# A GLA layer with its MLP on one core: the MLP as eight interleaved rounds, all of the down projection by sums, engine orders set in the source

## The chip, the core and the metric

The kernel runs on one core of a Trainium2 chip. The metric is the device time of one execution in microseconds. A core has a matrix engine (PE, whose weight loads are listed apart as PEld), three engines for elementwise work (DVE, ACT, POOL), and DMA queues that are fed by SP, ACT and POOL. Each engine takes its own instructions in the order in which they stand in its stream, and waits on semaphores for the others. PE writes into eight banks of PSUM of 128 x 512 float32; everything else lies in SBUF.

## The reference, cut to what matters

One layer: a chunked gated linear attention as the mixer, then an MLP with squared ReLU, then a final norm. 256 tokens, width 2048, hidden width 8192, all in float32. The change concerns the MLP.

```python
def _sq_relu_mlp(h, w_up, w_down):
    a = jax.nn.relu(h @ w_up)
    return (a * a) @ w_down

h = x
h = h + _gla_mixer(_rmsnorm(h, gla_norm), ...)
h = h + _sq_relu_mlp(_rmsnorm(h, mlp_norm), w_up, w_down)   # 256x2048 @ 2048x8192, then @ 8192x2048
return _rmsnorm(h, final_norm)
```

## The kernel before, in words

**Split numbers.** Every float32 operand of a large product is split into a high part (a cast on ACT to float32r, line 109) and a low part (the rest, a subtraction on DVE, line 110). A product of two such operands is three matmuls: high with high, high with low, low with high. Each matmul has a stationary block of 128 x 128 and 256 moving columns; the text calls one such matmul a product step.

**The mixer** (lines 180 to 560) projects with `natural` (line 142) and `turned` (line 157), each a loop that loads a piece of a weight matrix on SP's queue, splits it and multiplies. Small jobs of other kinds wait in the deque `side` and are let in by `pump` (line 88), one for each piece. The last jobs before the MLP turn the tokens: `turn` (line 510) transposes two blocks of 128 columns through an auxiliary bank on PE, and ACT and DVE write the high and low part of the turned `h`. `add_h` (line 542) adds the output projection to `h`, `ssq_h`, `scale2` and `scale2_row` (lines 548, 568, 576) make the norm's factor for each token as a row: squares on ACT, sums on DVE, a power on POOL, a diagonal on DVE, two small matmuls on PE.

**The MLP** goes in four rounds (`ROUNDS = HID // D`, line 61), each over 2048 hidden columns. A round first makes the up projection in four groups of 512 hidden columns (`up`, line 597, by `turned`), then the down projection in two halves of 1024 output columns (`down`, line 626). Per round, up is 4 x 192 = 768 product steps.

The down projection saves products by sums of blocks: tokens fall in two blocks of 128, hidden rows in pairs of blocks, output columns in pairs of 256. For such a 2x2 by 2x2 block product seven products of sums of blocks do instead of eight (lines 610 to 612 make the sums of the activations, line 666 those of the weights, line 686 and 697 put the results together from the banks `b32`, `b74`, `b16`, `b50`). Before the change only the left 512 of each 1024 output columns go that way; the right 512 (`blocks`, bank `plain`) are multiplied plainly. One pair of hidden blocks then takes 24 plain steps and 21 by sums:

```python
            product(b16, left, at(A11), w0, right, last)
            blocks(0, w0)
            product(b32, right, at(A12), w1, right, last)
            product(b32, left, at(S4), w1, left, last)
            blocks(1, w1)
            product(b50, left, at(S1), wu, slice(0, T), last)
            product(b74, left, at(S3), wu, slice(T, 2 * T), last)
            product(b16, right, at(S2), wu, slice(2 * T, 3 * T), last)
            product(b74, right, at(A22), wu, slice(3 * T, G), last)
```

In the second half, pair 0 is multiplied plainly (`PLAIN`, line 624), 48 steps. The very last half of the last round is all plain, and its last six pieces are held back so that the first token block's output can leave early (`last_step`, `held`).

**What sets the order.** Tile's scheduler orders the instructions of each engine by its own estimate of time and puts in all semaphores. `issue_after` ties the side jobs to the pieces. Split weights live in five buffers of 1024 columns (`wpool`), raw ones in three.

Of the kernel before, what the change touches and what calls it, by code (L numbers as in the profile page):

```python
# [27 lines left out]
F32 = mybir.dt.float32  # L28
# [32 lines left out]
ROUNDS = HID // D  # L61
# [5 lines left out]
def tile_gla_mlp(ctx, tc, x, xt, cols, w_vg, w_in, w_gate, w_out, w_up, w_down, final_norm, out):  # L67
# [3 lines left out]
    big = ctx.enter_context(tc.tile_pool(name="big", bufs=2))  # L71
    mid = ctx.enter_context(tc.tile_pool(name="mid", bufs=1))
    wpool = ctx.enter_context(tc.tile_pool(name="wpool", bufs=5))
    tmp = ctx.enter_context(tc.tile_pool(name="tmp", bufs=2))
    st = ctx.enter_context(tc.tile_pool(name="st", bufs=4))
    acc_p = ctx.enter_context(tc.tile_pool(name="acc_p", bufs=6, space=bass.MemoryType.PSUM))
# [114 lines left out]
    ones = const.tile([P, P], F32, name="ones")  # L191
    nc.vector.memset(ones, 1.0)
    warm = aux_bank()
    for _ in range(WARM):
# [4 lines left out]
    ident = const.tile([P, P], F32, name="ident")  # L199
# [4 lines left out]
    zz = big.tile([P, 2, 8, T], F32, tag="C", name="zz")  # L204
    kab = big.tile([P, 2, 8, T], F32, tag="C", name="kab")
    xth, xtl = (
        big.tile([P, KT * ROW + 64], F32R, tag="A" + i, name="x" + i, bufs=1)[:, OFF : OFF + KT * ROW]
# [93 lines left out]
    vh = big.tile([P, NT, D], F32R, tag="B", name="vh")  # L301
    vl = big.tile([P, NT, D], F32R, tag="B", name="vl")
    gn = const.tile([P, NT, GR], F32, name="gn")
# [21 lines left out]
    dq = const.tile([P, 8, 2], F32, name="dq")  # L325
# [107 lines left out]
    at = big.tile([P, 2, HEADS, 3 * P + 64], F32R, tag="C", name="at")  # L433
# [43 lines left out]
    on = big.tile([P, NT, D], F32, tag="C", name="on")  # L477
# [48 lines left out]
    oth, otl = (big.tile([P, KT * T + 128], F32R, tag="B", name="ot" + i) for i in "hl")  # L526
# [31 lines left out]
    hth, htl = (big.tile([P, KT, T], F32R, tag="A" + i, name="h" + i, bufs=1) for i in "hl")  # L558
# [26 lines left out]
    side.extend([scale2, nothing, scale2_row])  # L585

    A11, A12, A21, A22, S3, S1, S2, S4 = range(8)  # L590
    KP = KT // 2
    work = mid.tile([P, 3 * G + T], F32, tag="qt", name="work")
    r2row = work[:, 3 * G :]
    work = work[:, : 3 * G].rearrange("p (b c) -> p b c", b=3)
    ends = mid.tile([P, 4, T], F32, tag="db", name="ends")

    def up(r, q, act):
        acc = turned(hth, htl, w_up, r * D + q * GT, even=() if q > 1 or r > 0 and q else (5,) if r == q == 0 else (0,))
        flush()
        f = work[:, 2].rearrange("p (f s) -> p f s", f=8)  # L600
        for b in range(2):
            s = tmp.tile([P, 2, T], F32, tag="t512", name="su", bufs=3)
            nc.vector.scalar_tensor_tensor(
                s, acc[b].rearrange("p (i t) -> p i t", i=2), 0.0, r2row.unsqueeze(1).to_broadcast([P, 2, T]),
                op0=ALU.max, op1=ALU.mult,
            )
            nc.scalar.activation(
                f[:, :4].rearrange("p (t i) s -> p i t s", t=2), s.rearrange("p i (t s) -> p i t s", t=2), AF.Square
            )
            sub = lambda o, x, y: nc.vector.tensor_tensor(o, x, y, op=ALU.subtract)  # L610
            sub(f[:, S3 : S1 + 1], f[:, A21 : A21 + 1].to_broadcast([P, 2, P]), f[:, A11 : A22 + 1 : 3])
            sub(f[:, S2], f[:, A11], f[:, S1])
            sub(f[:, S4], f[:, A12], f[:, S2])
            oh, ol = (act[q][:, b, i].rearrange("p f s -> p (f s)") for i in range(2))
            nc.scalar.copy(oh, work[:, 2])
            nc.vector.tensor_tensor(ol, work[:, 2], oh.bitcast(F32), op=ALU.subtract)

    def stationary(act, kp, f):
        return [act[kp // 2][:, kp % 2, i, f] for i in range(2)]

    def take(bank, t, lo, n):
        nc.vector.tensor_tensor(h[:, t, lo : lo + n], bank, h[:, t, lo : lo + n], op=ALU.add)  # L622

    PLAIN = ((), (0,))

    def down(r, half, act):

        c0 = half * G
        plain = [aux_bank(), aux_bank()] if half == 0 else acc_banks(2)
        b32, b74 = acc_banks(2) if half == 0 else [aux_bank(), aux_bank()]  # L630
        b16, b50 = acc_banks(2)
        left, right = slice(0, T), slice(T, 2 * T)
        used = set()

        def product(bank, o, a, w, m, last):

            for i, (x, y) in enumerate(((0, 0), (0, 1), (1, 0))):
                halves(bank[:, o], a[x], w[y][:, m], bank.name not in used, last and i == 2)
                used.add(bank.name)

        for kp in range(KP):
            last = kp == KP - 1
            at = lambda f: stationary(act, kp, f)
            w = rows(w_down, c0, G, r * D)
            blocks = lambda i, wi: [
                product(plain[t], slice(0, 512), at((A11, A21)[t] + i), wi, slice(512, G), last and i == 1) for t in range(NT)
            ]
            if kp in PLAIN[half]:
                for i in range(2):
                    wi = weights(w(2 * kp + i), G)  # L650
                    blocks(i, wi)
                    product(b32, slice(0, 512), at(A11 + i), wi, slice(0, 512), False)
                    product(b50, right, at(A21 + i), wi, left, False)
                    product(b74, right, at(A21 + i), wi, right, False)
                    pump()
                continue
            assert not raw_half
            pair = wpool.tile([P, 2 * WMAX], F32, tag="raw", name="raw", bufs=3)
            raw0, raw1 = pair[:, :WMAX], pair[:, WMAX:]
            w0 = weights(w(2 * kp), G, skip=T, raw=raw0)  # L660
            product(b16, left, at(A11), w0, right, last)
            blocks(0, w0)
            pump()
            w1 = weights(w(2 * kp + 1), G, raw=raw1)
            u = work[:, kp % 2].rearrange("p (f s) -> p f s", f=4)
            add = lambda o, x, y: nc.vector.tensor_tensor(o, x, y, op=ALU.add)

            both = pair[:, T : T + 2 * (WMAX - T)].rearrange("p (k c) -> p k c", k=2)[:, :, :T]
            add(u[:, :2], raw0[:, left].unsqueeze(1).to_broadcast([P, 2, T]), both)
            add(u[:, 2], u[:, 0], raw1[:, left])  # L670
            add(u[:, 3], u[:, 2], raw1[:, right])
            wu = parts(work[:, kp % 2], G, slots())
            product(b32, right, at(A12), w1, right, last)
            product(b32, left, at(S4), w1, left, last)
            blocks(1, w1)
            product(b50, left, at(S1), wu, slice(0, T), last)
            product(b74, left, at(S3), wu, slice(T, 2 * T), last)
            product(b16, right, at(S2), wu, slice(2 * T, 3 * T), last)
            product(b74, right, at(A22), wu, slice(3 * T, G), last)
            if not last:  # L680
                pump()
        flush()
        for t in range(NT):
            take(plain[t], t, c0 + 512, 512)

        tt = lambda o, x, y: nc.vector.tensor_tensor(o, x, y, op=ALU.subtract)
        nc.scalar.copy(ends[:, 1], b16[:, left])
        tt(ends[:, 3], ends[:, 1], b16[:, right])
        tt(ends[:, 0], b50[:, left], ends[:, 3])
        tt(ends[:, 2], ends[:, 3], b74[:, left])  # L690
        take(b32, 0, c0, 512)
        take(b74, 1, c0, 512)
        if PLAIN[half]:
            take(b50[:, right], 1, c0, T)
        for t in range(NT):
            hv = h[:, t, c0 : c0 + 512].rearrange("p (i s) -> p i s", i=2)
            nc.vector.tensor_tensor(hv, hv, ends[:, 0 : t + 2 : t + 1], op=ALU.add)

    for r in range(ROUNDS):
        act = [big.tile([P, 4 * G + 64], F32R, tag="BC"[q // 2], name="act")[:, OFF:-16] for q in range(D // GT)]  # L700
        act = [a.rearrange("p (b i f s) -> p b i f s", b=2, i=2, f=8) for a in act]
# [102 lines left out]
```

## Time and profile before

| what | us |
|---|---|
| median of 3 runs | 1073.75 (1073.36 to 1073.92) |
| the profiled execution, span from its first to its last instruction | 1071.9 |
| PE busy in that span | 1062.2 |
| DVE busy | 780.3 |
| ACT busy | 576.7 |
| POOL busy | 12.7 |
| read from HBM | 206.92 MB, mean rate 195 GB/s |

The MLP's first product of the up projection starts 382.3 us into the span. A page of the profile is read as follows. "PE busy" counts matmuls that overlap each other, so the rate at which they start is the measure, and it is taken from the chain of waits, which lists merged stretches with their count. Groups are named by line, engine, operation, what is written and read, and shape; "x" is the count, then come the time busy in all and the mean duration of one. Consecutive instructions of DVE or ACT overlap a little, which the merged rows of the timeline show. DMA rows give the size of a transfer and the median time from issue to landing.

### The profile page before, as it was taken

The page shows a single profiled execution, that of the slowest core. Times are in us where ns is not written, and L with a number is a line of the kernel's source. Part 1 is how long each engine was busy: PE and PEld are TensorE (multiplying, and loading weights), DVE is VectorE, ACT ScalarE, POOL GpSimd, SP SyncE. Part 2 cuts the span into 40 slices and gives each one's busy share as a digit, 9 for nine tenths or more (in the row PEclk, how much of TensorE's full clock was granted, in tenths as well). Part 3 has the DMA queues.
Part 4 walks back from the last instruction along what each step waited for, and adds up shares of the span by engine and source line. Part 5 has one row for each costly group of instructions (what it writes and reads, how often), then busy time and mean ns, then how long its engine had stood idle before and what let it go on. Part 6 is the DMA issues. An engine that isn't in the chain of part 4 may idle for free.

```text
span 1071.9 us, 21858 instructions
## 1 busy us (share of the span) xinstructions
PE 1062.2 (99%) x9273; PEld 1061.5 (99%) x9273; DVE 780.3 (73%) x1039; ACT 576.7 (54%) x698; POOL 12.7 (1%) x39
## 2 busy tenths in 40 slices
PE   9999999999999999999999999999999999999997
PEld 9999999999999999999999999999999999999997
DVE  6668644546555566789986689986779997678974
ACT  7675444546444454556554556564556554555652
POOL 0000000000000000000000000000000000000000
PEclk9999999999999999999999999999999999999999
DMA  9856664556545555546566655566654666654662
GB/s 329 314 174 201 193 191 146 164 154 195 195 162 194 192 166 195 196 160 227 204 207 203 191 188 197 197 210 223 198 193 163 222 208 206 194 194 173 228 227 79
DMA packets 81009, 210.43 MB, mean 196 GB/s; under 512 B 6752, under 2 KB 9824, under 8 KB 80784
## 3 DMA queue, kind: packets, MB, share of 16 engines
q1 hardware_dynamic: 79808, 206.86, 58.8%
q10 hardware_dynamic: 1104, 2.19, 0.6%
q8 instruction: 72, 1.18, 0.4%
q14 instruction: 25, 0.20, 0.1%
HBM read 206.92 MB, written 2.10 MB: 195 GB/s over the span
## 4 chain that ended last, share of the span: by engine, by line
PE 98%; issue 1%; DMA 0%; DVE 0%; ACT 0%; SPq 0%; POOLq 0%; POOL 0%; DVEq 0%; ACTq 0%
PE acc L140 43%; PE acc L169 41%; PE aux L140 12%; PE aux L515 1%; PE aux L442 1%; DMA raw<-in_w_vg 0%; PE aux L343 0%; SPq L132 0%; DVE vl L307 0%; DVE hf L763 0%; ACT sqf L716 0%; DVE h L622 0%; ACT vh L306 0%; ACT hi L109 0%; POOLq L800 0%
## 5 line engine op out<-in xcount | busy, mean ns | idle before, releaser
L110 DVE TENSOR_TENSOR lo<-raw,hi 128x1024 fp32r<-128x1024 f32 (+3 forms) x386 | 453.2, 1176 | 231.1 <-ACT hi L109 228.9
L109 ACT CAST hi<-raw 128x1024 fp32r<-128x1024 f32 (+3 forms) x386 | 390.4, 1013 | 397.7 <-PE acc L169 172.6
L169 PE MATMUL acc<-hh,hi 128*128 128x256 f32 x1024 | 283.3, 277 | 0.0
L169 PE MATMUL acc<-hh,lo 128*128 128x256 f32 x1024 | 283.2, 277 | 0.0
L169 PE MATMUL acc<-hl,hi 128*128 128x256 f32 x1024 | 283.1, 276 | 0.0
L140 PE MATMUL acc<-hi,act 128*128 128x256 f32 x1194 | 217.1, 276 | 0.0
L169 PEld LDWEIGHTS acc<-hh,hi 128*128 128x128 f32 x1024 | 192.4, 188 | 0.0
L169 PEld LDWEIGHTS acc<-hh,lo 128*128 128x128 f32 x1024 | 192.4, 188 | 0.0
L169 PEld LDWEIGHTS acc<-hl,hi 128*128 128x128 f32 x1024 | 192.4, 188 | 0.0
L140 PEld LDWEIGHTS acc<-hi,act 128*128 128x128 f32 x1194 | 180.0, 188 | 0.0
L140 PE MATMUL acc<-lo,act 128*128 128x256 f32 x597 | 142.4, 276 | 0.0
L140 PE MATMUL aux<-hi,act 128*128 128x256 f32 x716 | 135.1, 276 | 0.0
L140 PEld LDWEIGHTS aux<-hi,act 128*128 128x128 f32 x716 | 107.9, 188 | 0.0
L140 PEld LDWEIGHTS acc<-lo,act 128*128 128x128 f32 x597 | 101.9, 188 | 0.0
L140 PE MATMUL acc<-lo,xh 128*128 128x256 f32 x480 | 77.5, 280 | 0.0
L140 PE MATMUL aux<-lo,act 128*128 128x256 f32 x358 | 76.9, 276 | 0.0
L140 PE MATMUL acc<-hi,xl 128*128 128x256 f32 x480 | 76.8, 279 | 0.0
L140 PE MATMUL acc<-hi,xh 128*128 128x256 f32 x480 | 76.0, 281 | 0.6 <-ACT hi L109 0.6
L109 ACT CAST hi<-work 128x1024 fp32r<-128x1024 f32 x53 | 56.0, 1056 | 32.0 <-PE aux L140 11.9
L110 DVE TENSOR_TENSOR lo<-work,hi 128x1024 fp32r<-128x1024 f32 x53 | 64.7, 1220 | 10.6 <-ACT hi L109 9.2
L169 PE MATMUL acc<-xh,hi 128*128 128x256 f32 x256 | 70.9, 277 | 0.4 <-DVE vl L307 0.4
L169 PE MATMUL acc<-xl,hi 128*128 128x256 f32 x256 | 71.0, 277 | 0.0
(137 smaller groups left out, 1266.2 us busy)
## 6 DMA issues: line engine op xcount, KB each, us to landing
raw<-in_w_up SPq DMA_DIRECT2D x128, 512.0 KB, 4.6
raw<-in_w_down SPq DMA_DIRECT2D x128, 512.0 KB, 4.4
raw<-in_w_in SPq DMA_DIRECT2D x80, 512.0 KB, 4.9
raw<-in_w_out SPq DMA_DIRECT2D x32, 512.0 KB, 4.4
raw<-in_w_vg SPq DMA_DIRECT2D x13, 520.0 KB, 8.0
h<-in_x SPq DMA_DIRECT2D x4, 512.0 KB, 7.1
zz<-in_xt SPq DMA_DIRECT2D x2, 512.0 KB, 9.6
fb<-in_final_norm ACTq DMA_DIRECT2D x1, 1024.0 KB, 6.7
```

The costliest lines, as they stand in the source:

```text
L109: last_hi[0] = nc.scalar.copy(hi[:, s], raw[:, s])
L110: last_lo[0] = nc.vector.tensor_tensor(lo[:, s], raw[:, s], hi[:, s].bitcast(F32), op=ALU.subtract)
L140: nc.tensor.matmul(o[:, m], x, w[:, m], start=first and c == 0, stop=last, skip_group_check=True)
L169: nc.tensor.matmul(o, u[:, s], m[:, kt], start=kt == 0 and n == 0 and j % 2 == 0, stop=kt == KT - 1 and n == 2, skip_group_check=True,)
L442: nc.tensor.matmul(o, kab[:, k[0], c0 + c, k[1] : k[1] + P], q(qt[:, c0 + c]), start=c == 0, stop=c == 1)
L515: nc.tensor.transpose(b[:, i * T + t * P : i * T + (t + 1) * P], src[:, t, kt * P : (kt + 1) * P], ident)
```

## The change

The MLP is written anew; in the mixer only the homes of some tiles move. What it does:

- There are eight rounds over 1024 hidden columns each (`ROUNDS = HID // G`), and all output columns go by sums. The last round's down projection (the last 1024 hidden rows) is plain. A step `d` of the down projection covers 512 hidden rows and 512 output columns: 24 product steps on weights as loaded and one sum among them (`raws`) and 18 on further sums (`summed`), 42 in all, 56 times. The plain rest is 8 x 48.
- The up projection goes in 64 pieces `u` of 512 x 512 (48 product steps). Nine pieces (`LEAD`) go ahead; then each cycle is 48 steps of up for a later round, 24 and 18 of down. A cycle has 90 product steps.
- One of the four sums of weights is made by a DMA on POOL's queue that adds one part of a raw tile into another (`accum_op`); DVE makes the other three, and splits them.
- The banks `b32`, `b74`, `b16`, `b50` are filled by ACT from their homes in SBUF (`h`, `kept`) before a visit to a stretch of 512 output columns and emptied back afterwards. At the end `combine` puts the parts together.
- Every job is put into `plan` with a time in product steps, relative to the product that needs it; the plan is sorted by time and run inside `tc.manual_schedule()`, which keeps that order on every engine.
- The split weights live in three slots of 2048 columns, the raw ones in two buffers for up and two for down, in a pool that takes the mixer's place (`mixer.close()`), with waits tile by tile.
- `turn` for the second half of `h`, `scale2` and `scale2_row` are plan entries at 6, 15, 24, 33, 48 and 72, between the up pieces at 0, 48 and 96.

```diff
-ROUNDS = HID // D
+ROUNDS = HID // G
+LEAD = 9
+UP, RAWS, SUMS = 24, 24, 18
+CYCLE = 2 * UP + RAWS + SUMS
...
     add_h(acc, G)
-    side.extend([lambda q=q: turn(h, row_h, g2, q) for q in range(4, 8)])
+    mixer.close()
+    mlp = ctx.enter_context(tc.tile_pool(name="mlp", bufs=1, reuse_waits="tile"))
...
+    SLOTS, PLACE = 3, 2 * G + 64
+    raw_u = [room_for(2 * G, f"rawu{i}") for i in range(2)]
+    slot = [[room_for(PLACE, f"{x}{i}", F32R) for x in ("high", "low")] for i in range(SLOTS)]
+    raw_d = [room_for(2 * G, f"rawd{i}") for i in range(2)]
...
+    T0 = 2 * UP * LEAD
+    cycle = lambda d: T0 + CYCLE * d
...
+    banks = acc_banks(6)
+    for q in range(4, 8):
+        at(6 + 9 * (q - 4), lambda q=q: turn(h, row_h, g2, q))
+    at(48, scale2)
+    at(72, scale2_row)
+    at(74, lambda: banks.__setitem__(slice(0, 0), [aux_bank(), aux_bank()]))
+    at(100, fold)
...
+    UP_LOAD, UP_HI, UP_LO = 120, 75, 56
...
+            def high(key=key, to=to, raw=raw):
...
+                nc.scalar.copy(to[0], raw)
...
+            def low(key=key, to=to, raw=raw):
...
+                nc.vector.tensor_tensor(to[1], raw, to[0].bitcast(F32), op=ALU.subtract)
...
+        chunk(("u", u), p - UP_HI, p - UP_LO, p + 2 * UP, (p - UP_LOAD, load), raw, 0 if u in SAME else OFF)
...
+    for g in range(GROUPS):
+        u = 4 * g + 3
+        e = up_time(u) + 2 * UP
+        for i in range(2):
+            at(e + 6 + i, lambda g=g, b=i: scaled(g, b))
+        steps = [lambda g=g: differ(g)] + [lambda g=g, b=b, f=f: f(g, b) for b in range(2) for f in (act_high, act_low)]
...
+        at(t - 30, lambda d=d: fill(d, B32))
+        at(t - 24, lambda d=d: fill(d, B16))
+        for i, run in enumerate((
+            lambda o=old, l=last: empty(o, B32, l), lambda d=d: fill(d, B50),
+            lambda o=old, l=last: empty(o, B50, l), lambda d=d: fill(d, B74),
+            lambda o=old, l=last: empty(o, B16, l), lambda o=old, l=last: empty(o, B74, l),
+        )):
+            at(t + 34 + 5 * i, run)
...
+            for f, name, o, a in ((3, B16, left, A11), (1, B32, right, A12), (0, B32, left, S4), (2, B50, left, S1)):
+                product(d, name, o, stationary(d, b, a), [x[:, f] for x in w])
...
+        for f, name, o, a in ((0, B16, right, S2), (1, B74, right, A22), (2, B74, left, S3)):
+            for b in range(2):
+                product(d, name, o, stationary(d, b, a), [s[:, f, b] for s in sums_to])
...
+            nc.sync.dma_start(out=raw.rearrange("p (i c) -> p i c", i=4), in_=src)
+            nc.gpsimd.dma_start(out=view[:, :, 1, left], in_=view[:, :, 1, right], accum_op=ALU.add)
+
+        chunk(("d", d), p - 67, p - 50, p + RAWS, (p - 143, load), raw)
+
+        def adds():
...
+            add(sums[:, 0], view[:, :, 1, left], view[:, :, 0, left])
+            add(sums[:, 1], sums[:, 0], view[:, :, 0, right])
+            sub(sums[:, 2], sums[:, 0], view[:, :, 1, right])
...
+            nc.scalar.copy(sums_to[0][:, f], sums[:, f])
...
+            sub(sums_to[1], sums, sums_to[0].bitcast(F32))
...
+        at(p - 68, adds)
+        at(q - 74, lambda: high(slice(0, 2)))
+        at(q - 65, lambda: high(2))
+        at(q - 54, low)
+        at(p, lambda: raws(d))
+        at(q, lambda: summed(d))
...
+    place_chunks()
+    with tc.manual_schedule():
+        for _, _, run in sorted(plan, key=lambda x: x[:2]):
+            run()
...
-    for kt in range(KT):
-        k = kt - KT + ROOM
-        w = weights(rows(w_down, G, G, (ROUNDS - 1) * D)(kt), G, room=k >= 0 and [room[:, i, k, :] for i in range(2)])
-        if kt < KT - LAST:
+    for kt in range(X_STEPS):
+        k = kt - X_STEPS + ROOM
+        piece = slice(kt % 2 * G, (kt % 2 + 1) * G)
+        to = [room[:, i, k, :] for i in range(2)] if k >= 0 else [s[:, piece] for s in slot[(taken + kt // 2) % SLOTS]]
+        w = weights(plain_source(X_STEPS + kt), G, room=to, raw=raw_u[kt // 2 % 2][:, piece])
+        if kt < X_STEPS - LAST:
```

More of the change, by code (lines that the diff above doesn't have):

```diff
@@ L583, in scale2_row @@
         nc.scalar.copy(r2row, b[:, :T])
[L585 to L600, printed above, removed]
-        for b in range(2):
[L602 to L682, printed above, removed]
-        for t in range(NT):
[L684 to L697, printed above, removed]
@@ new lines, in act_low @@
+    def act_low(g, b):
+        sub(act_part(g, b, 1), forms[:, b, span(g)], act_part(g, b, 0).bitcast(F32))
+        done.add(("act", g, b))
+    for g in range(GROUPS):
+        u = 4 * g + 3
+        e = up_time(u) + 2 * UP
+        for i in range(2):
+            at(e + 6 + i, lambda g=g, b=i: scaled(g, b))
+        steps = [lambda g=g: differ(g)] + [lambda g=g, b=b, f=f: f(g, b) for b in range(2) for f in (act_high, act_low)]
+        if u < LEAD:
+            times = (e + 24, e + 33, e + 42, e + 43, e + 54)
+        else:
+            c = lambda n: cycle(u - LEAD + n)
+            if g % 2 == 0:
+                times = (c(1) + 54, c(2) + 33, c(2) + 54, c(3) + 33, c(3) + 54)
+            else:
+                times = (c(0) + 66, c(1) + 33, c(1) + 54, c(2) + 33, c(2) + 54)
+        if g >= GROUPS - 2:
+            steps, times = steps[1:], (e + 46, e + 56, e + 57, e + 67)
+        for time, run in zip(times, steps):
+            at(time, run)
@@ new lines, in tile_gla_mlp, with home @@
+    PASS = [(c if r % 2 == 0 else 3 - c) for r in range(ROUNDS - 1) for c in range(4)]
+    starts = [d for d in range(SUMMED) if d == 0 or d % 2 == 0 and PASS[d // 2] != PASS[d // 2 - 1]]
+    first_of = {}
+    for d in starts:
+        first_of.setdefault(PASS[d // 2], d)
+    acc, written = {}, set()
+    B32, B74, B16, B50 = "b32", "b74", "b16", "b50"
+    def home(c, name):
+        cs = slice(c * GT, (c + 1) * GT)
+        return {B32: h[:, 0, cs], B74: h[:, 1, cs], B16: kept[:, c, 1:].rearrange("p f s -> p (f s)"), B50: kept[:, c, 0]}[name]
@@ new lines, in width, with fill, empty @@
+    def width(name):
+        return slice(0, T if name == B50 else GT)
+    def fill(d, name):
+        bank = banks.pop(0)
+        acc[d, name] = bank
+        c = PASS[d // 2]
+        if first_of[c] == d and name == B16:
+            return
+        written.add((d, name))
+        nc.scalar.copy(bank[:, width(name)], home(c, name))
+    def empty(d, name, last):
+        assert ("sums" if name in (B16, B74) else "raws", last) in done
+        bank = acc[d, name]
+        nc.scalar.copy(home(PASS[d // 2], name), bank[:, width(name)])
+        banks.append(bank)
@@ new lines, in tile_gla_mlp, with product @@
+    t = plain_time(2)
+    for n, name in enumerate((B32, B50, B16, B74)):
+        at(t + 4 * n + 2, lambda name=name: empty(starts[-1], name, SUMMED - 1))
+    left, right = slice(0, T), slice(T, GT)
+    def product(d, name, o, a, w):
+        s = visit(d)
+        bank = acc[s, name]
+        fresh = (s, name) not in written
+        written.add((s, name))
+        for i, (x, y) in enumerate(((0, 0), (0, 1), (1, 0))):
+            nc.tensor.matmul(
+                bank[:, o], a[x], w[y], start=fresh and i == 0, stop=d + 1 in starts + [SUMMED] and i == 2,
+                skip_group_check=True,
+            )
```

261 lines of the change are left out of this document (226 added, 35 removed).

## The prediction, made before the changed kernel was run

> **What bounds the kernel now.** I read the page's totals first, then the waits of PE, then the chain of waits in order of time.
>
> ```profile
> span 1071.9 us, 21858 instructions
> PE 1062.2 (99%) x9273; PEld 1061.5 (99%) x9273; DVE 780.3 (73%) x1039; ACT 576.7 (54%) x698; POOL 12.7 (1%) x39
> ...
> PE aux L195 <- DVE ones L192: 1.0, 1, 1.0
> PE acc L140 <- ACT hi L109: 0.6, 1, 0.6
> PE acc L169 <- DVE vl L307: 0.4, 1, 0.4
> ...
> 398.63 73.86 PE acc L169 x649
> 554.44 87.20 PE acc L169 x768
> 723.58 87.20 PE acc L169 x768
> ```
>
> PE never waits for longer than 1.0 us, and for 2.0 us in all. From 554.44 to 723.58 lies one whole round: 169.14 us for 768 steps of up and 360 + 363 of down, 1491 in all, so a step takes 0.1134 us, in up (87.20 / 768 = 0.1135) as in down. The kernel is bound by the number of product steps at that rate; a change pays in steps removed and costs what PE then waits. The profiled execution's span is 1071.9 us, 1.85 below the median of 1073.75; I sum on the span and add 1.85.
>
> **What it removes from PE.** Before: up 4 x 768 = 3072; down three rounds of 723 = 2169, and the last 360 + 384 = 744; 5985. After: up 64 x 48 = 3072; down 56 x 42 = 2352 and 8 x 48 = 384; 5808. The difference is 177 steps, x 0.1134 = **20.1 us**. Everything else must be paid from this.
>
> **Does DVE keep up?** A cycle of 90 steps gives every engine 90 x 0.1134 = 10.21 us. Durations by shape, from the groups by form:
>
> ```profile
> L110 DVE TENSOR_TENSOR lo<-raw,hi 128x1024 fp32r<-128x1024 f32 x313 | 382.5, 1223 | 216.8 <-ACT hi L109 215.6 <-issue 0.2
> L666 DVE TENSOR_TENSOR work<-raw 128x512 f32<-128x512 f32 x53 | 36.3, 685 | 1.9 <-DMA raw<-in_w_down 1.6
> L603 DVE SCALAR_TENSOR_TENSOR su<-acc,work 128x512 f32<-128x512 f32 x32 | 21.1, 688 | 0.0
> L610 DVE TENSOR_TENSOR work<-work 128x256 f32<-128x256 f32 x32 | 13.4, 418 | 0.0
> ...
> 1030.82 3.49 DVE L110 TENSOR_TENSOR lo<-raw,hi 128x1024 fp32r<-128x1024 f32 x3
> ```
>
> 512 more columns cost 1223 - 685 = 538 ns. So a low part of 2048 is 2.30 us (two in a cycle, for `u` and `d`: 4.60), that of the 1536 sums 1.76, the three sums 3 x 0.685 = 2.06: 8.42 a cycle. A group of hidden columns comes every four cycles: two `scaled` 1.38, `differ` 0.685 + 2 x 0.418 = 1.52, two low parts of 896 columns (1.09 each) 2.18; 5.08, or 1.27 a cycle. Together 9.69. Three low parts in a row took 3.49, not 3 x 1.223 = 3.67, so the sum shrinks by 5% to **9.2 us of 10.21**, 90%. The heaviest cycle holds `scaled` and an odd group's `differ`: (8.42 + 1.38 + 1.52) x 0.95 = 10.8, so 0.6 us run over into the next. What that meets: the low part of `d` is planned 2 steps before its cycle and needed 48 after it starts, 50 x 0.1134 = 5.7 us less its own 2.3, so 3.4 us of lead; `differ` also waits for ACT's two squares, perhaps 1 us. Some 2 us of lead remain, and the next cycles win it back. I take nothing for it.
>
> **Does ACT keep up?**
>
> ```profile
> L355 ACT ACTIVATE zz<-zz 128x2048 f32<-128x2048 f32 x1 | 1.9, 1917 | 0.0
> L109 ACT CAST hi<-work 128x1024 fp32r<-128x1024 f32 x53 | 56.0, 1056 | 32.0 <-PE aux L140 11.9 <-PE acc L140 11.1 <-PE acc L169 6.7
> L607 ACT ACTIVATE work<-su 128x512 f32<-128x512 f32 x32 | 20.1, 628 | 2.0 <-DVE act L616 2.0
> L306 ACT ACTIVATE vh<-acc,r 128x512 fp32r<-128x512 f32 x6 | 3.9, 688 | 0.9 <-PE acc L140 0.7
> L687 ACT COPY ends<-acc 128x256 f32<-128x256 f32 x7 | 2.6, 373 | 0.0
> ```
>
> Two high parts of 2048 (3.83), those of the sums (1.06 + 0.63), a quarter of a group's two squares and two casts of 896 (3.1 / 4 = 0.8): 6.3. New are the banks' moves. The 28 visits have 22 beginnings (six times the same stretch comes twice in a row); each fills and empties six times 512 and twice 256, 6 x 0.69 + 2 x 0.37 = 4.9 us by the rows of copies out of PSUM; copies into it the trace doesn't show, and 0.63 to 0.69 are the nearest from both sides. 22 x 4.9 / 56 = 1.9 a cycle; in all 8.2 of 10.21. The fills of `b50` and `b74` stand 9 and 23 steps (1.0 and 2.6 us) before the products and depend on nothing that PE still does, so ACT can run ahead. Nothing.
>
> **Loads, and the sum that a DMA makes.**
>
> ```profile
> raw<-in_w_up SPq DMA_DIRECT2D x128, 512.0 KB, 4.6
> zz<-in_xt SPq DMA_DIRECT2D x2, 512.0 KB, 9.6
> fb<-in_final_norm ACTq DMA_DIRECT2D x1, 1024.0 KB, 6.7
> out<-hf SPq DMA_DIRECT2D x4, 256.0 KB, 2.6
> ```
>
> A cycle loads 2 MB, 205 GB/s, near the 195 of before. Buffer `raw_d` is free when the low part of two steps earlier is read, about 18 us before the cycle; SP's queue holds only loads that become free earlier still. 1 MB lands in 6.7, at -11. Then POOL's accumulate of 256 KB must land before `adds`, planned 20 steps (2.3 us) before the cycle. No accumulate is in the trace; from both sides 2.6 (256 KB) and 9.6 (the slowest transfer of 512 KB): ready at -8.7 or at -1.7. The second is 0.6 late, within DVE's lead. I take 2.6; nothing in either case.
>
> **What the start of the MLP costs.** Here the plan puts on PE's stream: `u` 0, four turns, `u` 1, the norm's row, `u` 2. Nothing of PE stands between, whereas before these were let in one by one without a wait.
>
> ```profile
> 380.92 0.69 DVE L546 TENSOR_TENSOR h<-acc,h 128x512 f32<-128x512 f32 x1 [1.55 <-PE acc L140]
> 381.53 1.22 DVE L110 TENSOR_TENSOR lo<-raw,hi 128x1024 fp32r<-128x1024 f32 x1
> 382.66 1.88 DVE L546 TENSOR_TENSOR h<-acc,h 128x512 f32<-128x512 f32 x3
> ...
> 394.17 0.60 PE L515 MATMUL aux<-ident,h 128*128 128x128 f32 x4
> ...
> 394.43 0.85 ACT L520 ACTIVATE hh<-aux,colt 128x256 fp32r<-128x256 f32 x2 [1.32 <-DVE hl L521]
> ...
> 394.94 0.88 DVE L521 SCALAR_TENSOR_TENSOR hl<-aux,colt,hh 128x256 fp32r<-128x256 f32 x2 [0.54 <-ACT hh L520]
> ...
> L277 POOL TENSOR_TENSOR r<-ms,mhalf x4: 549/554/1513, 42.8 to 386.5; 128x1 f32<-128x1 f32 x4
> ```
>
> *Turns.* One takes 0.60 on PE, then from ACT's start (394.43) to DVE's end (395.82) 1.39; with a handover its bank is free after 2.1 us. Two auxiliary banks serve four turns: the third starts at 2.1 after the first, the fourth behind ACT's and DVE's next 0.9 at 2.9, and ends at 3.5. The four alone are about 1.5 of PE, as before. **Wait: 2.0 us.**
>
> *The norm's row.* After `u` 0 ends (0), ACT has two turns (0.7 to 2.4), the high part of `u` 2 (to 4.3), two turns (to 6.0), four squares at 0.61 each (to 8.5); DVE 0.4; POOL's two powers 1.1 to 2.0; DVE's diagonal 0.3, PE 0.4: 10.7 to 11.6. `u` 1 ran from 3.5 to 8.9, so with its own 0.4 PE waits 1.4 to 2.3, **1.9 us**.
>
> *The first low part* stands behind `add_h` in the source. In before DVE did such a one between two of those additions (381.53): the two are not ordered by data. I take 0; if it stood behind them, they end at 384.5 or, without the low part between, 383.6, and 2.3 later PE goes on: 385.9 against 382.5, 3.4.
>
> Together **3.9 us**. The end has the same held-back order with eight pieces instead of sixteen; its last low part comes, by loads of 4.6 and splits of 1.2, some 2 us before its product, so 0 to 2, and I take 0.
>
> **Sum:** 1071.9 - 20.1 + 3.9 = 1055.7, and with 1.85 **1057.6, say 1058 us**.
>
> **The rivals.** (a) *The first low part waits behind `add_h`*: 3.4 more, 1061. For it: the source order; against: the row at 381.53. 0.20. (b) *The start costs nothing*, 1054: only if the two chains above are shorter than the rows say. 0.08. (c) *A slower step.* The chain has stretches where a step takes 0.118:
>
> ```profile
> 342.59 2.83 PE acc L140 x24
> 387.06 5.07 PE acc L169 x43
> ```
>
> 2.83 / 24 = 0.1179. Nearly all steps of the MLP ran at 0.1134 before, though operands came from every buffer, which speaks against it; but all its operands, and some of the mixer's, now lie elsewhere. One such stretch of 24 in each of 55 cycles is 55 x 24 x 0.0045 = 6 us, 1064; all 5808 would be 26, 1084. 0.12, of which the first 0.09. (d) *Slower than before: DVE becomes the bound, because POOL's accumulate holds it.* DVE has 10.21 - 9.2 = 1.0 us to spare a cycle. If each accumulate kept it for x, every cycle grows by x - 1.0; the 16.2 us won are gone at 16.2 / 55 = 0.3, so from x = 1.3. Bounds: 0, and the whole 2.6 of a 256 KB transfer, 1.6 x 55 = 88 us. I price it at 1.5: 27, 1085. Against it stands the one place where POOL worked beside a low part:
>
> ```profile
> 386.02 2.03 POOL L277 TENSOR_TENSOR r<-ms,mhalf 128x1 f32<-128x1 f32 x2 [157.70 <-DVE ms L572]
> ...
> 386.42 1.22 DVE L110 TENSOR_TENSOR lo<-raw,hi 128x1024 fp32r<-128x1024 f32 x1 [0.48 <-ACT hi L109]
> ```
>
> Of the powers `r`, whose median is 0.55, one took 1.51 there, while DVE's 1.22 stayed 1.22: POOL waited. 0.11. [...] (e) *It doesn't do what it says*: the plan keeps less order than written and PE idles in cycles now and then, 1 to 12 us: 1064. 0.07.
>
> **How the numbers follow.** Forecast 0.42 (1055 to 1060), (a) 0.20, (b) 0.08, (c) 0.12, (d) 0.11, (e) 0.07. The range 1053 to 1070 leaves out (d) and the full (c), under 0.2. A measurement tells about 0.2% (2 us) from no change: faster is all but (d), the full (c) and some of (e), 0.83; same 0.04; slower 0.13.
>
> **What would show it.** PE's records fall by 177 to about 9096. In the cycles a step stays at 0.1134, so that eight cycles take 81.7 us; a wait of PE on `low` would speak for (d), steps of 0.118 without a wait for (c). DVE is busy about 90% there, ACT 75 to 80%. Two gaps of about 2 us stand around `u` 1, on a transposing matmul and on the diagonal; a third of 3.4 at 382 would be (a). POOL's accumulates land in about 3 us. I am wrong if PE waits in each cycle, however little: 0.3 us a cycle eat all.

## The result, and the profile after: slower, at one lasting rate

The changed kernel took **1090.6 us** (four runs, 1089.7 to 1092.2); before took 1073.6 on the same chip. The ratio is 1.0159, with an interval from 1.0145 to 1.0173. The forecast was 1058, with a range up to 1070. The profiled execution's span grew from 1071.9 to 1089.3, by 17.4. One run of e1 (1092.8 us) and one of s2 (1090.8) below stand apart as slow runs, about as long as the changed kernel's; they have no trace and are left out of the times given there.

First the page of the changed kernel: totals, then one group and a row of the DMA issues.

```profile
span 1089.3 us, 21348 instructions
PE 1071.9 (98%) x9096; PEld 1069.8 (98%) x9096; DVE 817.5 (75%) x832; ACT 663.2 (61%) x798; POOL 80.4 (7%) x96
...
L881 POOL DMA_DIRECT2D rawd<-rawd x56 | 67.7, 1210 | 540.9 <-DVE sums L869 214.2
...
rawd<-rawd POOLq DMA_DIRECT2D x56, 256.0 KB, 5.5
```

PE's records fell by 177, as forecast, and yet its busy time grew. That alone says that a step, not a wait, became dearer. PE's waits (us in total, times, longest):

```profile
PE acc L719 <- DVE low L682: 3.1, 1, 3.1
PE aux L522 <- DVE hl L528: 2.6, 2, 1.8
PE acc L844 <- DVE low L682: 1.2, 1, 1.2
...
PE aux L643 <- DVE diag L642: 0.8, 2, 0.6
```

Line 719 is the up projection, 844 the products of down, 522 a turn, 643 the norm's row. Together 7.7. Every one of these lies at the start of the MLP or at the first step of down; three others, 2.0 together as in before, lie in the first 54 us. In the 55 cycles behind that, PE waits for nothing. The chain of waits of the same kernel (start, us, what) shows the last wait and what came behind it:

```profile
430.56 6.72 DMA rawd<-in_w_down
437.60 10.03 DMA rawd<-rawd
453.92 5.10 PE acc L844 x41
459.01 5.65 PE acc L719 x48
...
1020.81 5.65 PE acc L719 x48
```

A piece of up takes 5.65 from 459 to beyond 1020: 5.65 / 48 = 0.1177 a step, against 0.1134 before. The windows (length; busy time of PE, PEld, DVE, ACT and POOL with counts; granted clock; DMA share; GB/s) say the same in counts, and add something at the start:

```profile
388.80:392.20 3.40, 3.40 (x18) 3.40 (x17) 0.97 (x1) 0.00 (x0) 0.00 (x0) 0.51 0.93 340
399.10:402.40 3.30, 3.30 (x17) 3.30 (x16) 1.36 (x3) 2.17 (x5) 0.00 (x0) 0.50 0.00 0
425.30:452.40 27.10, 27.10 (x242) 27.10 (x241) 15.52 (x15) 12.91 (x13) 2.55 (x2) 1.00 0.81 252
454.20:1010.00 555.80, 555.80 (x4721) 555.80 (x4721) 491.38 (x407) 384.99 (x420) 63.98 (x53) 1.00 0.79 224
```

In the cycles 4721 steps fall in 555.80 us, 0.1177 each, with the clock at 1.00. Just before, from 425.3 to 452.4, 239 steps of the up projection started in 27.10 us (the counts of the window take in some that began earlier), 0.1133 each, also at 1.00. DVE is busy 88% of the cycles, ACT 69%: neither is the bound.

Where the 17.4 us come from, by the starts of all steps, each taken against 0.1134:

| part | us |
|---|---|
| 177 steps fewer | -20.1 |
| the mixer (first step of up at 384.1, was 382.3) | +1.8 |
| start of the MLP to the first step of down: 11.7 above the rate, was 0.7 | +11.0 |
| the wait at the first step of down, 452.5 | +1.4 |
| 5325 steps at 0.1178 from 454.1 to the end | +23.3 |

The parts add up to the 17.4. Of the mixer's 1.8, 1.4 arises between 304 and 344 us, and it is the same rise of the step, in the mixer's own products. Here is one window of both kernels, first before, then the changed one:

```profile
310.00:341.00 31.00, 31.00 (x276) 31.00 (x275) 15.78 (x15) 11.44 (x12) 0.00 (x0) 1.00 0.60 201
310.00:341.00 31.00, 31.00 (x266) 31.00 (x265) 15.32 (x15) 11.53 (x11) 0.00 (x0) 1.00 0.52 183
```

By their starts that is 0.1133 a step in before and 0.1178 in the changed kernel, with no wait of PE ahead of it in either.

### The profile page after: what moved, and what is told of

Read it like the earlier page. It is cut to its first block, busy times and chain, and to the rows that moved or that the text cites. A ratio compares the mean times of both kernels' runs of the same rounds, so it can differ in the third digit from the quotient of the medians.

```text
span 1089.3 us, 21348 instructions
## 1 busy us (share of the span) xinstructions
PE 1071.9 (98%) x9096; PEld 1069.8 (98%) x9096; DVE 817.5 (75%) x832; ACT 663.2 (61%) x798; POOL 80.4 (7%) x96
## 4 chain that ended last, share of the span: by engine, by line
PE 79%; issue 17%; DMA 2%; DVE 1%; ACT 0%; POOL 0%; SPq 0%; POOLq 0%; DVEq 0%; ACTq 0%
PE acc L719 27%; PE acc L844 18%; PE acc L146 13%; PE acc L175 8%; PE aux L844 8%; PE aux L719 3%; PE aux L146 2%; DMA rawd<-rawd 1%; DMA rawd<-in_w_down 1%; PE aux L449 1%; DMA raw<-in_w_vg 0%; DVE low L682 0%; ACT hi L115 0%; DVE forms L980 0%; DVE h L869 0%
## 5 line engine op out<-in xcount | busy, mean ns | idle before, releaser
L719 PE MATMUL acc<-hh,low 128*128 128x256 f32 x896 | 251.3, 280 | 3.1 <-DVE low L682 3.1
L719 PE MATMUL acc<-hl,high 128*128 128x256 f32 x896 | 252.0, 281 | 0.0
L719 PE MATMUL acc<-hh,high 128*128 128x256 f32 x896 | 251.4, 281 | 0.0
L116 DVE TENSOR_TENSOR lo<-raw,hi 128x1024 fp32r<-128x1024 f32 (+4 forms) x132 | 157.3, 1193 | 124.2 <-ACT hi L115 123.8
L115 ACT CAST hi<-raw 128x1024 fp32r<-128x1024 f32 (+4 forms) x132 | 135.0, 1025 | 139.5 <-PE acc L146 92.1
L719 PEld LDWEIGHTS acc<-hh,low 128*128 128x128 f32 x896 | 169.0, 189 | 3.3 <-DVE low L682 3.3
L719 PEld LDWEIGHTS acc<-hh,high 128*128 128x128 f32 x896 | 170.0, 190 | 0.0
L719 PEld LDWEIGHTS acc<-hl,high 128*128 128x128 f32 x896 | 169.6, 189 | 0.0
L682 DVE TENSOR_TENSOR low<-rawu,high 128x2048 fp32r<-128x2048 f32 x68 | 155.6, 2289 | 17.7 <-ACT high L677 15.7
L677 ACT CAST high<-rawu 128x2048 fp32r<-128x2048 f32 x68 | 129.2, 1902 | 15.3 <-PE aux L719 7.8
```

Source lines behind the costliest of these rows:

```text
L115: last_hi[0] = nc.scalar.copy(hi[:, s], raw[:, s])
L116: last_lo[0] = nc.vector.tensor_tensor(lo[:, s], raw[:, s], hi[:, s].bitcast(F32), op=ALU.subtract)
L677: nc.scalar.copy(to[0], raw)
L682: nc.vector.tensor_tensor(to[1], raw, to[0].bitcast(F32), op=ALU.subtract)
L719: nc.tensor.matmul(o, w[:, s], m[:, kt], start=kt == 0 and n == 0 and j % 2 == 0, stop=kt == KT - 1 and n == 2, skip_group_check=True,)
```

## The experiments

Theory A says that PE's step has two rates that last: a pause of PE puts it to 0.118, and it stays there until something ends it. In before that something would be a piece of up whose split weights stand at the head of their buffer: `even` in `turned` gives such a piece offset 0, all others `OFF = 48` columns, and the first piece of each later round of the MLP is one (in the first round it is piece 5 of the first group and the first piece of the second). The changed kernel has them only at `u` 2 and 4 (`SAME`). Theory B says that the new addresses or the new order of products make the step slow. Theory C says it is the chip's granted clock.

### e1: one piece at offset 0 after the slow stretch has begun

```diff
-    SAME = (2, 4)
+    SAME = (2, 4, 12)
```

> The changed kernel with one more piece of up (12) whose weights stand at offset 0, as pieces 2 and 4 do, after which the trace of after has steps of 0.113. Theory A (a gap on PE puts the step to 0.118 and it stays so until such a piece): the 1.4 us wait at the first step of down remains, some 300 steps at 0.118, the 48 of piece 12 at 0.120, then about 4970 steps at 0.1134: 4970 x 0.0044 = 22 us less, about 1068. Theory B (the rate follows from where the new operands lie, or from up and down taking turns): only the 48 steps change, 1090.5. Theory C (the granted clock fell after the idle time): 1090.5 and the clock stays below 1.

Measured: 1069.3 us, ratio to before 0.9966 (0.9951 to 0.9981). The chain of e1:

```profile
463.18 4.95 PE acc L844 x42
468.12 5.65 PE acc L719 x48
...
478.72 5.75 PE acc L719 x48
...
489.24 5.44 PE acc L719 x48
```

Down ran at 4.95 / 42 = 0.1179 and up at 0.1177, the piece at offset 0 at 0.1198, and the next piece of up at 0.1133. One number in a tuple takes 21 us off, and the layout and the order of the other 5,000 products are as they were. In this execution the first step of down came but 0.11 us late (the 42 steps from 452.47 take 5.06, those from 463.18 take 4.95), and the slow rate had still begun there.

### e2: take away the wait that began it

The load of `d` = 0 is issued earlier (150 steps into the plan instead of 143 before its step), so that its accumulate lands in time.

```diff
-        chunk(("d", d), p - 67, p - 50, p + RAWS, (p - 143, load), raw)
+        chunk(("d", d), p - 67, p - 50, p + RAWS, (p - 143 if d else 150, load), raw)
```

> The changed kernel with the load of the first down step's weights planned at 150 instead of 337, so that its accumulate lands before it is needed; nothing else moves. Theory A: the wait of 1.4 us at the first step of down goes, PE keeps the 0.1134 that it has from 425 us on through all cycles, 23.3 + 1.4 less: about 1066. Theory B: the wait goes, the steps stay at 0.118: 1089. Theory C: as A where the clock is the cause of the 0.118, but with the clock at 1.

Measured: 1067.1, ratio 0.9942 (0.9928 to 0.9957). The window of e2 that answers to the last one of the changed kernel:

```profile
454.20:1010.00 555.80, 555.80 (x4906) 555.80 (x4905) 502.08 (x419) 397.94 (x436) 65.19 (x54) 1.00 0.79 229
```

185 steps more in the same 555.80 us: 0.1133 each, through every buffer and the whole new order of products. **B falls.** The clock is 1.00 in both windows: **C falls.** DVE is 90% busy here. At the end of the same trace the timeline shows the slow rate behind another small delay:

```profile
1010.57 0.39 PE L146 MATMUL aux<-high,act 128*128 128x256 f32 x2
1010.80 0.50 PE L146 MATMUL acc<-low,act 128*128 128x256 f32 x2
1011.14 0.40 PE L146 MATMUL aux<-low,act 128*128 128x256 f32 x2
```

One step is 0.11 late; the 24 behind it, from 1011.14 to 1013.97, take 0.118 each.

### e3: no piece at offset 0 in the MLP, on top of e2

```diff
-    SAME = (2, 4)
+    SAME = ()
```

> The changed kernel with the early load (1067.1), and no piece of up at offset 0. Theory A': the gaps at the start put the step to 0.118 and nothing ends it: 240 + 5170 steps more at 0.0044 = 23.5 us, less the 0.6 of the two pieces at 0.120: about 1090. If the step recovered by itself once PE is fed again: 1066.5.

Measured: 1091.2, ratio 1.0164 (1.0150 to 1.0177). The same window of e3:

```profile
454.20:1010.00 555.80, 555.80 (x4722) 555.80 (x4721) 488.87 (x405) 384.48 (x420) 63.98 (x53) 1.00 0.78 223
```

Without such a piece the rate that the start leaves, 0.1177, stays for some 5,700 steps to the end. In this run nothing else ended it.

### b1 to b4: the same in the kernel before

Before runs at 0.1133 from 410 us on, but for 24 steps at 0.120 at the head of each round. b1 puts four idle transposes ahead of the second group of up of the second round; b2 does so and makes the group's first piece one at offset 0.

```diff
+        if r == 1 and q == 1:
+            b = aux_bank()
+            for i in range(4):
+                nc.tensor.transpose(b[:, i * P : (i + 1) * P], h[:, 0, i * P : (i + 1) * P], ident)
```

> The kernel of before with four transposes by PE, into a bank that nobody reads, put ahead of the second group of up in the second round. Theory A: from there to the first piece of the third round's up, which stands at offset 0 (about 576 + 723 = 1300 steps), the step is 0.118: 1300 x 0.0044 = 5.7 us, and 0.5 for the transposes: about 1080. Theory B: the layout is that of before, only the transposes cost: 1074.2. Theory C: as B.

> The same kernel, with the piece of weights just behind the transposes at offset 0. Theory A: 24 steps at 0.120 and then 0.1134 again: about 1074.5, 5.5 below the kernel without it. Theory B: 1074.4, as without it.

Measured: 1074.6 and 1074.8, ratios 1.0009 (1.0000 to 1.0018) and 1.0011 (1.0002 to 1.0020). For b1 that is a miss: the rate did not change, as its chain shows (65.29 / 576 = 0.1133):

```profile
578.53 65.29 PE acc L169 x576
```

So these four transposes were not enough. b3 therefore makes PE pause: a second transpose needs ACT's copy of the first, and the products are tied behind it. b4 is the same with the next piece at offset 0.

```diff
+            nc.tensor.transpose(b[:, :P], h[:, 0, :P], ident)
+            nc.scalar.copy(back, b[:, :P])
+            last = nc.tensor.transpose(b[:, P : 2 * P], back, ident)
+            after.enter_context(tc.issue_after(last.ins))
```

> The kernel of before; ahead of the second group of up in the second round PE makes one transpose, ACT copies its result, and PE has to wait for that copy for a second transpose, with all further products behind it: a gap of about 1 us, without any change of the layout. Theory A' (a gap puts the step to 0.118, transposes between products alone need not): some 1300 steps at 0.118 up to the third round's first piece at offset 0: 5.7 us and 1.2 for the gap, about 1080.7. Theory B (the changed kernel's layout or order of products made its 0.118): only the gap, 1075.

> The same with the first piece of weights behind the gap at offset 0. Theory A': 24 steps of 0.120, then 0.1134 again: 1.2 for the gap and 0.2: about 1075.2. Theory B: 1075, as without it.

Measured: b3 1081.5, ratio 1.0064 (1.0046 to 1.0082); b4 1075.7, ratio 1.0012 (1.0003 to 1.0022). The chain of b3:

```profile
577.95 67.84 PE acc L169 x576
...
730.94 87.19 PE acc L169 x768
```

After the pause a step takes 67.84 / 576 = 0.1178, in up and in down, until the next round begins with its piece at offset 0; then 87.19 / 768 = 0.1135. A pause in which PE waits 1.1 us for ACT's copy, with its two transposes, costs 7.4 us in an untouched layout. In b4 the piece behind the pause ends the slow rate within its 24 steps (the 196 steps from 577.67 take 22.36, 0.1141 each), and 1.6 us remain. **A stands** in these runs: behind a late step a step took 0.118 (e1, e2, b3), and behind a piece at offset 0 it took 0.113 again (e1, b3, b4). But the slow rate also began without a wait of PE. In before, that of the start of the MLP begins at 384.0 us, behind one transposing matmul at 383.78 for which PE waited for nothing; that of the 31 us of the changed kernel's mixer above begins behind four at 303.98, without a wait as well; behind b1's four it did not begin. In b3, transposes and pause stand together, and which of them began it is not shown. The late steps of the changed kernel, e1 and e2 have no transpose ahead of them.

### e4: is it the offset? On top of e2

```diff
-        chunk(("u", u), p - UP_HI, p - UP_LO, p + 2 * UP, (p - UP_LOAD, load), raw, 0 if u in SAME else OFF)
+        chunk(("u", u), p - UP_HI, p - UP_LO, p + 2 * UP, (p - UP_LOAD, load), raw, 16 if u in SAME else OFF)
```

> The changed kernel with the early load, and pieces 2 and 4 at an offset of 16 float32 (64 bytes) instead of 0. If it takes weights and moving tokens at the same offset to end the 0.118: as without, about 1090. If any other offset than 48 does: 1067. If a smaller distance than 192 bytes is enough: 1067 with steps of 0.120 in these pieces.

Measured: 1066.5, ratio 0.9927 (0.9911 to 0.9942). The traced run is the slowest of five (1071.1; the others 1065.3 to 1066.7). Its chain, pieces 2 and 3, then 4 on:

```profile
408.53 12.58 PE acc L719 x96
421.12 8.95 PE aux L719 x79
```

Pieces 2 and 3 take 12.58, where in e2, with piece 2 at offset 0, they take 11.19; whether piece 2 at offset 16 ended the slow rate these totals do not show. From piece 4 on, at offset 16 too, a step takes 8.95 / 79 = 0.1133, without the steps of 0.120 (0.1198 in e1) that a piece at offset 0 takes. So with these pieces at offset 16 the slow rate did not last (1066.5 against the 1091.2 of e3), and piece 4 did not cost what one at offset 0 does; which addresses end the slow rate stays open.

### s1 to s4: the waits at the start, all on top of e2

s1 moves `add_h` of the second half into the plan, 6 steps ahead of the first product, and so behind the first low part on DVE. s2 spreads the turns and moves the norm. s3 does both, and more. s4 is s3 with three more pieces at offset 0.

```diff
+    at(-6, lambda: add_h(out_banks, G))                       # s1, s3, s4
+    at(-5, lambda: banks.extend(acc_banks(6)))                # s1, s3, s4
-        at(6 + 9 * (q - 4), lambda q=q: turn(h, row_h, g2, q))
+        at((6, 15, 54, 63)[q - 4], lambda q=q: turn(h, row_h, g2, q))   # s2, s3, s4
-    at(48, scale2)
-    at(72, scale2_row)
+    at(66, scale2)                                            # s2, s3, s4
+    at(120, scale2_row)                                       # s2; s3 and s4: 190
-        chunk(("p", j), p - 60, p - 42, p + 2 * UP, (p - 110, load), raw)
+        chunk(("p", j), p - (60 if j else 66), p - 42, p + 2 * UP, (p - 110, load), raw)   # s3, s4
-    SAME = (2, 4)
+    SAME = (2, 4, 12, 28, 44)                                 # s4
```

> The changed kernel with the early load of the first down step (that alone: 1067.1), and the additions of the output projection to h moved in the source behind the low parts of pieces 0 and 1. If the order of the source held those low parts back, PE's wait of 3.3 us at the first piece goes, and with it the half-speed clock behind it, 17 steps at 0.1 more each, 1.7 us: about 1062. If DVE was late for another reason: 1067.

s1 measured 1061.8, ratio 0.9882 (0.9863 to 0.9900), as expected. Its waits and three windows of it:

```profile
PE aux L522 <- DVE hl L528: 2.6, 2, 1.8
PE aux L643 <- DVE diag L642: 2.4, 2, 1.8
```

```profile
390.30:394.40 4.10, 1.55 (x13) 1.13 (x12) 1.84 (x4) 2.97 (x5) 0.00 (x0) 1.00 0.00 0
394.40:399.70 5.30, 5.30 (x48) 5.30 (x47) 3.29 (x5) 4.16 (x12) 0.00 (x0) 1.00 0.00 0
...
420.00:1040.00 620.00, 620.00 (x5472) 620.00 (x5472) 555.59 (x475) 436.10 (x479) 66.40 (x55) 1.00 0.78 228
```

The wait for the first low part is gone, and the clock stays at 1.00 through and behind the turns. The diagonal, which had partly hidden behind the half clock, now makes PE wait for 2.4 (0.8 in the changed kernel). From 420 to 1040 a step takes 620.00 / 5472 = 0.1133.

> The changed kernel with the early load (1067.1), and with turns 6 and 7 behind piece 1 instead of ahead of it, the norm's sums at 66 and its row behind piece 2. If the two auxiliary banks and the norm's chain made the waits: 1.9 + 0.95 of the turns and about 0.8 of the diagonal go, and the 1.5 of half-speed steps behind them: about 1062. If something else did: 1067.

s2 measured 1065.4, ratio 0.9917 (0.9898 to 0.9936): a miss. The waits of the turns went, and that of the diagonal grew to 3.5:

```profile
PE aux L643 <- DVE diag L642: 3.5, 1, 3.5
```

> The changed kernel with all three: the early load of the first down step, the additions to h behind the first two low parts, turns 6 and 7 behind piece 1; and the norm's row behind piece 3 (190), since the diagonal still held PE for 3.5 us at 120; the first plain piece's high part 6 steps earlier. Against s1_first (1061.8) the 2.85 of the turns and the 1.9 of the diagonal go: about 1057. Theory B would have no reason for it to stay below 1062.

> The same with the pieces 12, 28 and 44 of up also at offset 0. Theory A': each costs 48 steps x 0.0066 = 0.3 us, 0.9 more in an undisturbed execution, about 1058; what it buys is that an execution with a stray gap in the cycles does not stay at 0.118 to the end (23 us).

s3 measured 1064.5, ratio 0.9920 (0.9907 to 0.9933); s4 1066.6, ratio 0.9935 (0.9922 to 0.9947). s3 misses its 1057 by 7.5, and s4 is no better. The largest wait of PE in both traces, 4.3 us, is for the diagonal, here in the timeline of DVE of s3:

```profile
413.47 2.29 DVE L684 TENSOR_TENSOR low<-rawu,high 128x2048 fp32r<-128x2048 f32 x1 [4.05 <-ACT high L679]
415.68 0.48 DVE L642 TENSOR_SCALAR diag<-square,r 128x128 f32<-128x128 f32 x2
```

The diagonal stands behind a low part that itself waited 4.05 for ACT, whose cast had waited 5.99 for a load and began only at 411.54. Put later in the plan, the diagonal is behind more work in DVE's fixed order. It is not the whole miss: in both traces PE also waits 1.8 for a low part and 0.9 for a high part, and the mean granted clock of the two is 0.996 and 0.995, against 0.998 in s1's. Three more pieces at offset 0 bring nothing (1066.6 against 1064.5).

### s5: the norm early instead of late

On top of s1: the turns as in s2; `scale2` at 1, the diagonal at 16 and the norm's two matmuls at 52, into a bank that stands free, so that neither DVE nor PE has anything late in front of them; the splits of pieces 2 and 3 are moved out of the way, and the first plain piece is split earlier, as in s3.

```diff
-    at(48, scale2)
-    at(72, scale2_row)
+    at(1, scale2)
+    at(16, norm_diag)
+    at(52, norm_sums)
+    at(64, norm_row)
...
-        chunk(("u", u), p - UP_HI, p - UP_LO, p + 2 * UP, (p - UP_LOAD, load), raw, 0 if u in SAME else OFF)
+        chunk(("u", u), {2: -3, 3: 50}.get(u, p - UP_HI), {2: 3, 3: 53}.get(u, p - UP_LO), p + 2 * UP, (p - UP_LOAD, load), raw, 0 if u in SAME else OFF)
```

> From s1_first (1061.8): turns 6 and 7 behind piece 1; the squares for the norm ahead of the turns, where ACT is idle, the diagonals right behind, the norm's two products behind piece 1, its row copied behind the last turn; the high and low parts of pieces 2 and 3 ahead of the turns, so that their buffers are loaded again in time. If the waits at the start come from the order in which the plan puts these on ACT and DVE, all of 2.85 (turns) and 2.0 (diagonal) go: 1057. If they come from the loads of pieces 4 and 5 (which s3_all had late by 6 us), they reappear as a wait of pieces 4 or 5: 1060 to 1064.

Measured: **1055.2 us, ratio 0.9827 (0.9814 to 0.9840)**: faster than both kernels, and below the 1057 expected. The chain of s5 at the start of the MLP and in the cycles:

```profile
384.20 5.44 PE acc L732 x48
389.64 0.87 PE aux L522 x8
390.51 5.66 PE acc L732 x48
396.17 0.44 PE acc L649 x4
396.62 0.87 PE aux L522 x8
397.49 11.19 PE acc L732 x96
...
987.00 5.44 PE acc L732 x48
```

Nothing but PE's own work is left in the chain here: up, two turns, up, the norm's row, two turns, up. Steps of 0.118 are left in two places. One is the piece behind the first two turns (5.66 / 48 = 0.1179), once more without a wait of PE; piece 2, at offset 0, ends it. The other is in the chain from 993 to 1039, by 0.0045 a step some 2 us in all.

## Why the prediction was wrong, point by point

- **Fewer steps: right.** 177 fewer records. With the waits gone, s5's span of 1055.4 (its traced run is the slowest of five) is 16.5 below that of before: 20.1, less 1.8 of the mixer and about 2 of its slow end.
- **"A step takes 0.1134 us, in up as in down": right for before, wrong as a rate of the changed kernel.** This is the step that failed, and it cost 23.3 us. Rival (c) at its full size, priced at +26 and given 0.03, is what happened. My reason against it was that the steps of before ran at 0.1134 "though operands came from every buffer". That compared addresses, where the cause is history: whether a late step has begun the slow rate, and whether a piece that ends it came after (e1, e2, e3). Before has such a piece at the head of each round; the changed kernel has its last one at `u` 4, and a wait of 1.4 us behind that. The stretch of 43 steps at 0.118 that I quoted from before, 387.06, stands right behind six transposing matmuls of the turns, in PE's timeline of before:

```profile
386.24 0.82 PE L515 MATMUL aux<-ident,h 128*128 128x128 f32 x6
```

  The steps had come 0.118 apart since 384, and they did so until a piece at offset 0 at 399. I listed the stretch and did not ask where that rate began and where it ended.
- **The accumulate by DMA: its size was off.** I took 2.6 us; the median is 5.5. The first took the 10.03 of the chain above, just over my upper bound of 9.6. I had called both ends harmless by DVE's lead. In the cycles that was so. At the first step it was not. Its cycle starts 48 steps ahead of 452.5, at 447.0. The load was issued 16.5 ahead of that and landed 9.8 ahead, where I had 18 and 11, and the accumulate landed 0.6 behind it, where my later bound had 1.7 ahead. I had also let only DVE's sums wait for it; ACT's cast of the same tile waited too, and so did the low part that DVE makes from that cast. The timelines of SP's queue, POOL, ACT and DVE show the way from the load to PE:

```profile
430.56 0.46 SPq L880 DMA_DIRECT2D rawd<-in_w_down  x1
```

```profile
437.60 1.34 POOL L881 DMA_DIRECT2D rawd<-rawd  x1 [29.72 <-DMA rawd<-in_w_down]
```

```profile
447.78 1.92 ACT L677 CAST high<-rawd 128x2048 fp32r<-128x2048 f32 x1 [3.25 <-DMA rawd<-rawd]
```

```profile
447.65 0.69 DVE L869 TENSOR_TENSOR sums<-rawd 128x512 f32<-128x512 f32 x1 [2.79 <-DMA rawd<-rawd]
...
451.57 2.28 DVE L682 TENSOR_TENSOR low<-rawd,high 128x2048 fp32r<-128x2048 f32 x1
```

- **DVE and ACT keep up: right.** 88 to 90% and 69 to 72% in the cycles (the changed kernel and e2), forecast 90 and 75 to 80, and no wait of PE in them.
- **Rival (d), POOL holds DVE: wrong.** By the operations on `rawd` (duration min, median, max in ns) DVE's low part is even, 2.28 to 2.29 us, although 17 of the 56 ran while POOL issued an accumulate. That an accumulate holds DVE was my assumption, and no run shows it. Rival (e) is wrong too: PE waits for nothing in the cycles.

```profile
L682 DVE TENSOR_TENSOR low<-rawd,high x56: 2282/2285/2294, 451.6 to 1025.5; 128x2048 fp32r<-128x2048 f32 x56
```

- **The start, 3.9 forecast, 11.0 found.** Rival (a) was true as well. In DVE's timeline of the changed kernel the first low part stands behind all four additions of `add_h`, and PE's timeline has the gap:

```profile
382.72 2.65 DVE L553 TENSOR_TENSOR h<-acc,h 128x512 f32<-128x512 f32 x4 [9.71 <-PE acc L146]
385.29 4.48 DVE L682 TENSOR_TENSOR low<-rawu,high 128x2048 fp32r<-128x2048 f32 x2
```

```profile
384.22 0.28 PE L719 MATMUL acc<-hl,high 128*128 128x256 f32 x1
387.63 0.38 PE L719 MATMUL acc<-hh,low 128*128 128x256 f32 x1 [3.13 <-DVE low L682]
```

  That is 3.3 of PE, by (a) 3.4. That before did such a low part between two additions showed that data allow it, not that the new source order does it. The turns cost 2.9 instead of 2.0. The diagonal cost 0.8 instead of 1.9, but only because PE was slower in front of it: in s1 it is 2.4. And the clock fell to 0.51 and 0.50 for 3.4 and 3.3 us, about 3 us together, which no term of the sum had. The last 1.0 of the 11.0 is steps at 0.118 and 0.120.
- **The last steps and the loads: right.** No wait of PE stands at the end of the changed kernel. At the fast rate small delays come up: in e2 a step 0.11 late at 1010.80, with steps of 0.118 behind it, and in e4 two waits that the changed kernel does not have, 0.6 in down (line 844) and 0.8 in the last products (line 146).

## What to carry to other kernels

A rate read from a steady stretch holds only while what made it holds, so find in the trace where each rate begins and ends before carrying it over. A wait that is short by itself can stand ahead of a slower rate of everything behind it (here 1.4 us ahead of 23.3), so first take away the wait that stands ahead of the longest undisturbed stretch. In an order fixed in the source, a small job that PE needs must stand early on its engine; put later, it came behind more work (PE waited 3.5 in s2 and 4.3 in s3), put early it cost nothing (s5).

## What the runs showed of the hardware

- **Two lasting rates of the same product step** (128 x 128 by 256 columns, float32r): 0.1133 and 0.118 us, both at a granted clock of 1.00 (the windows from 454.20 to 1010.00 of e2 and of the changed kernel). The slow one followed a step of down or of the last products that came 1.4 us late in the changed kernel and 0.11 in e1 and e2, without a transpose ahead of it. Behind transposes without a wait it began in some places (before, s5) and not in others (b1). Some 5,700 steps did not end it (e3); in e1, b3, b4 and s5 it had ended behind a piece with weights at offset 0, which itself took 0.1198 a step in e1. Why, and by which addresses, is open (e4).
- **The granted clock halved twice at the start of the changed kernel's MLP.** It was 0.51 from 388.80 to 392.20 and 0.50 from 399.10 to 402.40; between the two, from 392.20 to 394.60, and from 402.50 to 406.40 it was 1.00. The first drop came 1.1 us after PE had resumed from a wait of 3.13, as the row of 387.63 shows; ahead of the second PE had waited 1.76 and 0.79 for the turns (2.6 together). In s1 PE waited the same 2.6 for the turns, and from 386.00 to 402.00 the clock stayed at 1.00. How much idle time makes the clock fall, the runs do not show.
- **An accumulate of 256 KB from SBUF to SBUF on POOL's queue** lands in 5.5 us (median of 56 in the changed kernel), longer than the loads of 1024 KB beside it take (5.1), and occupies POOL for 1.21.
